# A two-layer decoder on one core: layer 1's expert values as 64 gathered columns and 4 whole chunks, with the list work spread wider

## The chip, the cores and the metric

The kernel runs on one core of a Trainium2 chip. The metric is the device time of one execution in microseconds (us). A core has a matrix engine (TensorE; PE in the profile, with PEld for its weight loads), VectorE (DVE), ScalarE (ACT), GpSimd (POOL) and SyncE (SP). Each engine works through its own list of instructions in order, and semaphores make it wait for the others. SP, ACT and POOL can issue DMA transfers. Products are accumulated in eight PSUM banks; all other data of the engines lie in SBUF.

## What is computed

Input `x` has 256 tokens of width 1024. Each of two layers mixes tokens (layer 0 an mLSTM, layer 1 an RG-LRU, both with cross attention to 256 memory tokens), adds and normalizes, and then applies a mixer of 16384 experts (PEER). The change is about that mixer:

```python
def peer_ffn(x, w_q, subkeys, u_tab, v_tab):      # blocks of 128 tokens
    def block(xb):
        q = (xb @ w_q).reshape(n, PEER_HEADS, 2, PEER_HALF)
        s = jnp.einsum('nhpc,pkc->nhpk', q, subkeys)
        sv, si = lax.top_k(s, PEER_TOPK)
        ...
        fv, fi = lax.top_k(cand.reshape(n, PEER_HEADS, PEER_TOPK * PEER_TOPK), PEER_TOPK)
        eid = ...                                 # ids of 16 experts for each of 8 heads
        gw = jax.nn.softmax(fv, axis=-1)
        act = gelu(jnp.einsum('nhkd,nd->nhk', u_tab[eid], xb))
        return jnp.einsum('nhk,nhkd->nd', gw * act, v_tab[eid])
```

Each token uses 128 of the 16384 experts. Everything is float32, and the tables `u_tab` and `v_tab` hold 16384 rows of 1024 numbers a layer.

## The kernel before

**Tiling.** The experts are 128 chunks of 128 (an expert is a chunk and a partition). A float32 product is made of three faster ones (`mm3`, L310 to L312): high part by high part, high by low and low by high. ACT casts a loaded tile to its high part (L193), and DVE (L208) or POOL (L206) subtracts to get the low part. `pool_cols` says how many columns of it POOL takes.

**First half of the mixer (u).** For every chunk TensorE computes all 256 tokens against its 128 rows of `u` (`u_step`, 256 wide), ACT applies gelu, and DVE multiplies with the gate weights from the top-k selection (L1571). The result, one 128x256 block of coefficients per chunk, stands in `wglo` (chunks 0 to 43) and `wghi` (44 to 127). The chunks of the last 20 steps are called `h` = 64 to 83 in the loop in front of the value phase.

**Second half (v).** The output is the sum over experts of coefficient times row of `v`. Most experts are used by few tokens or none, so the kernel doesn't multiply all 128 chunks. In layer 1 ("joint" in the code) the first `nj` chunks are written to a table in DRAM, `joined`: a row is an expert's 128 coefficients of token block 0, its 1024 values of `v`, and its 128 coefficients of block 1. SP copies the values in, 512 KB a chunk, with every second call of `next` from the first weight load of the kernel on (L286); ACT and SP write the coefficients (`dump`, eight chunks at a time; the two last groups by SP). `lists` (L1142 on) then ranks the used rows of every partition on DVE and writes row numbers to `crow`. A *column* is 128 used rows, one per partition, that one indirect DMA by POOL fetches from `joined` (L248): for one token block 128x1152 numbers, for both 128x1280. There are 15 places for them in `wghi`. Of each partition 16 rows for each block and 8 for both go straight into columns; what is left over (room for `over` rows a partition) is packed into further, "spilled" columns, whose row numbers come from a one-hot product: ten-odd DVE comparisons (L1306) make the one-hots, four left-over rows at a time, and 36 TensorE products (L1313) select. If the left-overs don't fit, a branch computes all chunks in full (`dense`). The chunks from `nj` on are *dense* items: SP loads their whole `v` rows, and they count for both token blocks.

**The value phase.** The loop `for i in range(NC)` takes the items in the order of `value_order`. Item by item ACT casts (L193), DVE subtracts (L208), ACT and DVE split the coefficients (L365, L366), and TensorE multiplies: six products of 128x512 for a token block (two halves of 512 columns, three products each), so six for a single column and twelve for a column of both blocks or a dense chunk. They accumulate in four PSUM banks.

**What sets the order around the change.** Instructions are issued to each engine in the order in which the program writes them. The list work is a generator that is stepped by `tail_lists`: each tick has a budget (`LIST_US` a tick until the rows are ranked, `REST_US` after), and each step is written with the time it takes. A tick comes with every u-step `h` and every value item `i` until the lists are done. Fetching begins when the rows are ranked and the dumps are issued (`self.vrow = self.crow`), and from then on the subtractions go to DVE.

```python
                    self.dumped = n >= len(DUMPS) - 1
                    self.listed = not lists
                    if joint and self.dumped and self.ranked:
                        self.vrow = self.crow
```

Of the kernel before, what the change touches and what calls it, by code (L numbers as in the profile page):

```python
# [7 lines left out]
F32 = mybir.dt.float32  # L8
# [10 lines left out]
P = 128  # L19
# [17 lines left out]
class Shape:  # L37
# [8 lines left out]

    def blocks(self, col):
# [21 lines left out]
SPARE_AT = (P, 14)  # L69
# [10 lines left out]
def value_order(kept, sh):  # L80
    short = list(range(sh.side)) + list(range(sh.a_end, sh.a_end + sh.side))
    short += list(range(sh.side, sh.b_beg)) + list(range(sh.a_end + sh.side, sh.cols))
    both = list(range(sh.b_beg, sh.a_end))
    dense = list(range(sh.nj, P))
    nb = (kept + 1) // 2
    both, last = both[:-nb], both[-nb:]
    dense, spare = dense[:len(dense) - kept + nb], dense[len(dense) - kept + nb:]
    n, ns, cols = len(short) + len(both), len(short), []
    for k in range(n):
        more = (k + 1) * ns // n > k * ns // n  # L90
        cols.append((short if more else both).pop(0))
    out, t = [], 0.0
    for k, c in enumerate(cols):
        while dense and t < sh.first_us + k * sh.pair_us:
            out.append((dense.pop(0), None))
            t += ITEM_US
        t = max(t, sh.first_us + k * sh.pair_us) + ITEM_US * len(sh.blocks(c)) / 2
        out.append((None, c))
    out += [(c, None) for c in dense]
    return out + [(None, last.pop(0)) if k % 2 == 0 else (spare.pop(0), None) for k in reversed(range(kept))]  # L100
# [26 lines left out]
class Trunk:  # L127
# [123 lines left out]
    def fetch(self, dst, col):  # L251
        rows = self.vrow[:, col:col + 1]
        if self.sh.joint:
            n = P * len(self.sh.blocks(col)) + D
# [20 lines left out]
    def next(self, ahead=HL_BUFS):  # L275
# [8 lines left out]
        if self.copying and self.copies and self.calls % 2 == 0:  # L284
# [857 lines left out]
    def lists(self, layer):  # L1142
# [6 lines left out]
        def take(*shape, dt=F32):  # L1149
# [4 lines left out]
            assert at[0] <= (24 if sh.joint else 20) * T  # L1154
            v = v if dt is F32 else v.bitcast(dt)
# [19 lines left out]
        q16, z_in, W = take(OVER, dt=F16), take(OVER, dt=F16), take(OVER, 2, dt=F16)  # L1175
# [118 lines left out]
        nc.vector.tensor_copy(q16, qi2)  # L1294
# [9 lines left out]
        for r in range(0, OVER, 4):  # L1304
            full = [P, 4, P]
            tt_(Q[:, r:r + 4], self.iota2[:, :, 0].unsqueeze(1).to_broadcast(full),  # L1306
                q16[:, r:r + 4].unsqueeze(2).to_broadcast(full), op=ALU.is_equal)
# [33 lines left out]
    def peer_layer(self, layer):  # L1341
# [3 lines left out]
        with ExitStack() as ctx:  # L1345
# [5 lines left out]
            self.crow = wg.tile([P, WIDTH], I32, name="crow")  # L1351
            self.vids = wg.tile([P, WIDTH], I32, name="vids")
# [128 lines left out]
            def tail_lists():  # L1481
                lists = self.lists(layer)
                marks = [c for g in ACT_GROUPS[layer] for c in range(8 * g, 8 * g + 8)]
                budget, n = 0.0, 0
                while True:
                    gain = REST_US if self.ranked else LIST_US
                    budget = min(budget + gain, gain)
                    if n < len(DUMPS):
                        self.dump(nc.scalar, 8 * DUMPS[n], 8, CUT, T)
                    if joint and n in LATE_DUMPS:  # L1490
                        self.dump(nc.sync, 8 * LATE_DUMPS[n], 8, 0, T)
# [12 lines left out]
                    self.dumped = n >= len(DUMPS) - 1  # L1504
# [56 lines left out]
            side = tail_lists()  # L1561
            prev = None
            self.pool_cols, self.chained = D, False
            cs = [] if joint else [coef(0), coef(1)]
            for h in range(NS, NH + 1):
# [9 lines left out]
                if joint and h == NS + 15:  # L1575
# [23 lines left out]
            for i in range(NC):  # L1599
# [3 lines left out]
                if not closed:  # L1603
                    next(side)
# [221 lines left out]
```

## Time and profile before

| | before |
|---|---|
| runs (us) | 1450.7, 1446.2, 1440.04; median 1446.2 |
| the profiled execution (us) | 1449.33 |
| its span (us) | 1447.6 |
| mean TensorE clock granted | 0.996 of full |
| TensorE busy | 1415.5 us |
| DVE busy | 1174.2 us |
| layer 1's value phase | first product at 1302.89, last at 1439.95 |
| block-units there | 50 single columns + 2x12 columns of both + 2x8 dense = 90 |

The span runs from the first to the last instruction of the profiled execution; the device time holds 1.7 us more. Times inside the trace count from the start of the span. In rows of a timeline stand start, duration, engine, line, operation, tiles and count, and in brackets how long the engine idled before it and what ended that. In rows of windows stand, for each stretch, the busy time of TensorE, its weight loads, DVE, ACT and POOL (with instruction counts), the granted clock, the busy share of the DMA engines, and GB/s. In rows of groups stand busy time, mean duration in ns, idle time before, and its releaser.

### The profile page before, as it was taken

The page shows a single profiled execution, that of the slowest core. Times are in us where ns is not written, and L with a number is a line of the kernel's source. Part 1 is how long each engine was busy: PE and PEld are TensorE (multiplying, and loading weights), DVE is VectorE, ACT ScalarE, POOL GpSimd, SP SyncE. Part 2 cuts the span into 40 slices and gives each one's busy share as a digit, 9 for nine tenths or more (in the row PEclk, how much of TensorE's full clock was granted, in tenths as well). Part 3 has the DMA queues.
Part 4 walks back from the last instruction along what each step waited for, and adds up shares of the span by engine and source line. Part 5 has one row for each costly group of instructions (what it writes and reads, how often), then busy time and mean ns, then how long its engine had stood idle before and what let it go on. Part 6 is the DMA issues. An engine that isn't in the chain of part 4 may idle for free. (4 is left out here: it accounts for less than half of the span.)

```text
span 1447.6 us, 30077 instructions
## 1 busy us (share of the span) xinstructions
PE 1415.5 (98%) x11043; PEld 1334.9 (92%) x11043; DVE 1174.2 (81%) x2676; ACT 896.0 (62%) x1937; POOL 592.0 (41%) x500
## 2 busy tenths in 40 slices
PE   8999999999999999999999989999999999998997
PEld 7989999999999999888889879999999999996786
DVE  4667577979999998777886774978899999878986
ACT  4546455555559985566755925555555799845883
POOL 2100665003333349677730136710223323678740
PEclk9999999999999999999999999999999999999999
DMA  8858768887779999889848547788775689997981
GB/s 271 304 201 305 242 228 291 293 287 251 239 248 281 265 242 290 322 301 329 309 152 300 196 150 264 262 291 281 273 239 171 196 261 255 254 321 294 402 342 66
DMA packets 184277, 378.83 MB, mean 262 GB/s; under 512 B 66338, under 2 KB 100140, under 8 KB 183868
## 3 DMA queue, kind: packets, MB, share of 16 engines
q1 hardware_dynamic: 109720, 283.31, 59.2%
q0 software_dynamic: 18608, 69.94, 13.0%
q10 hardware_dynamic: 55796, 23.61, 6.1%
q8 instruction: 88, 1.44, 0.4%
q14 instruction: 65, 0.53, 0.1%
HBM read 346.38 MB, written 93.33 MB: 304 GB/s over the span
## 5 line engine op out<-in xcount | busy, mean ns | idle before, releaser
L310 PE MATMUL bank<-xHL,wH 128*128 128x256 f32 x2536 | 719.3, 284 | 1.9 <-ACT wH L193 1.9
L312 PE MATMUL bank<-xHL,wL 128*128 128x256 f32 x2536 | 708.2, 279 | 6.1 <-DVE wL L208 5.8
L311 PE MATMUL bank<-xHL,wH 128*128 128x256 f32 x2536 | 707.2, 279 | 1.8 <-DVE xHL L366 1.7
L193 ACT CAST wH<-raw 128x1024 fp32r<-128x1024 f32 (+3 forms) x385 | 396.0, 1031 | 369.3 <-PE bank L311 126.8
L312 PEld LDWEIGHTS bank<-xHL,wL 128*128 128x128 f32 x2536 | 478.9, 189 | 9.1 <-DVE wL L208 8.0
L311 PEld LDWEIGHTS bank<-xHL,wH 128*128 128x128 f32 x2536 | 479.3, 189 | 2.6 <-DVE xHL L366 2.6
L310 PEld LDWEIGHTS bank<-xHL,wH 128*128 128x128 f32 x2536 | 477.7, 188 | 2.9 <-ACT wH L193 2.7
L208 DVE TENSOR_TENSOR wL<-raw,wH 128x1024 fp32r<-128x1024 f32 (+3 forms) x186 | 205.5, 1109 | 136.6 <-ACT wH L193 134.4
L206 POOL TENSOR_TENSOR wL<-raw,wH 128x1024 fp32r<-128x1024 f32 (+1 forms) x97 | 212.4, 2194 | 227.2 <-ACT wH L193 225.0
L203 POOL TENSOR_TENSOR wL<-raw,wH 128x386 fp32r<-128x386 f32 x128 | 131.2, 1025 | 291.3 <-DVE wL L201 286.1
L1084 DVE TENSOR_TENSOR oh<-iota,i12T 128x1024 f16<-128x1024 f16 x128 | 138.7, 1084 | 0.0
L312 PE MATMUL bank<-wH,cL 128*128 128x512 f32 (+1 forms) x339 | 133.2, 393 | 2.8 <-DVE cL L366 2.8
L310 PE MATMUL bank<-wH,cH 128*128 128x512 f32 (+1 forms) x339 | 132.7, 391 | 2.8 <-ACT cH L365 2.6
L311 PE MATMUL bank<-wL,cH 128*128 128x512 f32 (+1 forms) x339 | 132.9, 392 | 0.6 <-DVE wL L208 0.6
L201 DVE TENSOR_TENSOR wL<-raw,wH 128x640 fp32r<-128x640 f32 x128 | 105.6, 825 | 14.7 <-ACT wH L193 10.4
L208 DVE TENSOR_TENSOR wL<-wghi,wH 128x1024 fp32r<-128x1024 f32 x66 | 80.8, 1223 | 24.7 <-ACT wH L193 24.6
L248 POOL DMA_INDIRECT wghi<-joined,crow x62 | 85.3, 1376 | 22.5 <-issue 15.5
L1087 DVE TENSOR_TENSOR oh<-oh,gT 128x1024 f16<-128x1024 f16 x128 | 90.0, 703 | 4.4
L193 ACT CAST wH<-wghi 128x1024 fp32r<-128x1024 f32 x66 | 69.3, 1051 | 37.8 <-PE bank L312 25.0
L312 PEld LDWEIGHTS bank<-wH,cL 128*128 128x128 f32 x339 | 63.9, 189 | 19.6 <-DVE cL L366 6.2
L1463 PE MATMUL bank<-oh 128*128 128x128 f16 x1024 | 81.1, 220 | 0.0
L310 PEld LDWEIGHTS bank<-wH,cH 128*128 128x128 f32 x339 | 64.0, 189 | 16.5 <-ACT cH L365 3.1
(371 smaller groups left out, 2095.2 us busy)
## 6 DMA issues: line engine op xcount, KB each, us to landing
raw<-in_u_dram SPq DMA_DIRECT2D x256, 512.0 KB, 4.2
joined<-in_v_dram SPq DMA_DIRECT2D x120, 512.0 KB, 5.5
raw<-in_w_q_dram SPq DMA_DIRECT2D x32, 512.0 KB, 4.0
raw<-in_v_dram SPq DMA_DIRECT2D x20, 512.0 KB, 5.5
raw<-in_w_out_dram SPq DMA_DIRECT2D x16, 512.0 KB, 5.1
raw<-in_w0qx_dram SPq DMA_DIRECT2D x8, 512.0 KB, 5.4
wghi<-in_v_dram SPq DMA_DIRECT2D x8, 512.0 KB, 6.0
raw<-in_w1x_dram SPq DMA_DIRECT2D x8, 512.0 KB, 4.1
```

Source lines behind the costliest of these rows:

```text
L193: (nc.vector.tensor_copy if self.cast_dve else nc.scalar.copy)(h[:, c], r[:, c])
L201: nc.vector.tensor_sub(l[:, k:], r[:, k:], h[:, k:].bitcast(F32))
L203: nc.gpsimd.tensor_sub(l[:, :k], r[:, :k], h[:, :k].bitcast(F32))
L206: nc.gpsimd.tensor_sub(l[:, :k], r[:, :k], h[:, :k].bitcast(F32))
L208: nc.vector.tensor_sub(l[:, k:], r[:, k:], h[:, k:].bitcast(F32))
L248: self.nc.gpsimd.indirect_dma_start(out=dst, out_offset=None, in_=table, in_offset=bass.IndirectOffsetOnAxis(ap=rows, axis=0))
L310: mm(out, sH, mH, start=start, stop=False, skip_group_check=True)
L311: mm(out, sH, mL, start=False, stop=False, skip_group_check=True)
L312: mm(out, sL, mH, start=False, stop=stop, skip_group_check=True)
L1084: nc.vector.tensor_tensor(flat(oh[:, 1:3]), self.iota2.unsqueeze(1).to_broadcast([P, 4, P, 2]), pairs(self.i12T[:, j]), op=ALU.is_equal)
L1087: nc.vector.tensor_tensor(flat(oh[:, 0:2]), two.rearrange("p z (q e t) -> p z q e t", q=2, t=2), pairs(self.gT[:, j]), op=ALU.mult)
L1463: nc.tensor.matmul(wp[:, qs], oh[:, 2, q // 2, :, q % 2], oh[:, z, q // 2, :, q % 2], start=z == 0, stop=z == 1, skip_group_check=True)
```

## The change

**Shape.** `nj` goes from 120 to 124, the room for left-over rows from 36 to 40 a partition, and the spilled columns from (9, 9, 4) to (9, 10, 5): 51 single columns, 13 of both, 4 dense chunks. The list vectors widen from 120 to 124 and from 36 to 40, the comparisons go from 9 to 10, the index products from 36 to 40.

**Order of the value items.** Before: dense 120 and 121, then a column of both and five or six single ones in turn, 122 to 125 at items 61 to 64, and columns of both alternating with dense 126 and 127 at the end. After: dense 124 and 125, then the long items (126, 127 and the columns of both) dealt out evenly among the single ones (one both at item 2, 126 at item 9, the next both at 16, ..., 127 at 49), and at the end six columns of both. The first spilled column is item 40 in both orders.

**Pace of the list work.** `REST_US` is 1.2 instead of 1.0, and in layer 1's value loop the gain is 0.4 with a single column and 1.2 with a long item. The lists end with item 16 instead of 10.

**The comparison's operand.** `q16` (float16, SBUF) becomes `qp` (float32, in a PSUM bank), in both layers.

**Copies.** No copy of `v` into `joined` goes before the 16th call of `next`; four more chunks are copied, so the copying goes on longer in both layers (`COPY_END` 40).

**Dumps and fetching.** SP dumps chunks 120 to 123 as well, in tick 17, and fetching waits for it: it begins in the tick of `h` = 81 instead of 78, and the first coefficient splits come at `h` = 82 instead of 79. Four more marks of used rows fall to ACT, the spare buffers come into use from item 26 instead of 14, and the row numbers of both layers share one tile, `words`.

```diff
-SHAPES = (Shape(104, 16, 8, 28, (5, 6, 3), 5.0, 2.8, False), Shape(120, 16, 8, 36, (9, 9, 4), 3.0, 1.6, True))
-WIDTH = 62
+SHAPES = (Shape(104, 16, 8, 28, (5, 6, 3), 5.0, 2.8, False), Shape(124, 16, 8, 40, (9, 10, 5), 3.0, 1.75, True))
+COPY_AT = 16
+DENSE_FIRST = 10
-LIST_US, REST_US, LOOK = 2.25, 1.0, 10
-ACT_GROUPS = ((5, 9), (5, 9, 13))
+LIST_US, REST_US, LOOK = 2.25, 1.2, 10
+REST_HALF = 0.4
+ACT_GROUPS = ((5, 9), (5, 9, 13, 15))
-LATE_DUMPS = {6: 13, 12: 14}
-COPY_END = 33
+LATE_DUMPS = {6: 13, 12: 14, 17: 15}
+COPY_END = 40
-SPARE_AT = (P, 14)
+SPARE_AT = (P, 26)
...
+    if sh.joint:
+        out = [(dense.pop(0), None) for _ in range(2)]
+        long = [(None, c) for c in cols if len(sh.blocks(c)) == 2]
+        cols = [c for c in cols if len(sh.blocks(c)) == 1]
+        for k in range(len(dense)):
+            long.insert((2 * k + 1) * len(long) // (2 * len(dense)) + k, (dense[k], None))
+        n, m, dense = len(long), len(cols), []
+        for k in range(m):
+            if k * n // m > (k - 1) * n // m:
+                out.append(long.pop(0))
+            out.append((None, cols[k]))
+        out, cols = out + long, []
...
-        if self.copying and self.copies and self.calls % 2 == 0:
+        if self.copying and self.copies and self.calls >= COPY_AT and self.calls % 2 == 0:
...
-        nc.vector.tensor_copy(q16, qi2)
+        qp = self.bank()[:, :OVER]
+        nc.vector.tensor_copy(qp, qi2)
...
-                q16[:, r:r + 4].unsqueeze(2).to_broadcast(full), op=ALU.is_equal)
+                qp[:, r:r + 4].unsqueeze(2).to_broadcast(full), op=ALU.is_equal)
...
-                    gain = REST_US if self.ranked else LIST_US
-                    budget = min(budget + gain, gain)
+                    gain = self.gain if self.ranked else LIST_US
+                    budget = min(budget + gain, max(gain, REST_US))
...
-                        self.dump(nc.sync, 8 * LATE_DUMPS[n], 8, 0, T)
+                        self.dump(nc.sync, 8 * LATE_DUMPS[n], min(8, NJ - 8 * LATE_DUMPS[n]), 0, T)
...
-                    self.dumped = n >= len(DUMPS) - 1
+                    self.dumped = n >= (max(LATE_DUMPS) if joint else len(DUMPS) - 1)
...
-                if joint and h == NS + 15:
+                if joint and h == NJ - N0 + 2:
                     cs = [coef(0), coef(1)]
...
+                    if joint:
+                        self.gain = REST_HALF if len(blocks(order[i][1])) == 1 else REST_US
                     next(side)
```

**Where instructions move: the value phase's start on DVE.** `wL<-raw` is the low part of a loaded chunk, `wL<-wghi` that of a gathered column, `cL` that of coefficients, `wghi<-wghi,bank` the gate product of a u-step, and `wglo<-iota` a comparison. Before, from the last but one u-step on:

```order
L1571 TENSOR_TENSOR wghi<-wghi,bank 128x256
L1306 TENSOR_TENSOR wglo<-iota_93,wglo 128x512 x2
L1571 TENSOR_TENSOR wghi<-wghi,bank 128x256
L208 TENSOR_TENSOR wL<-wghi,wH 128x1024
L1306 TENSOR_TENSOR wglo<-iota_93,wglo 128x512
L366 TENSOR_TENSOR cL<-wghi,cH 128x256
L208 TENSOR_TENSOR wL<-wghi,wH 128x1024
L1306 TENSOR_TENSOR wglo<-iota_93,wglo 128x512
L366 TENSOR_TENSOR cL<-wghi,cH 128x128
L208 TENSOR_TENSOR wL<-wghi,wH 128x1024
```

After, at the same place (line numbers are some 20 higher):

```order
L1594 TENSOR_TENSOR wghi<-wghi,bank 128x256
L1323 TENSOR_TENSOR wglo<-wglo 128x40x24
L1327 TENSOR_TENSOR wglo<-iota_93,bank 128x512
L1594 TENSOR_TENSOR wghi<-wghi,bank 128x256
L227 TENSOR_TENSOR wL<-wghi,wH 128x1024
L1327 TENSOR_TENSOR wglo<-iota_93,bank 128x512
L386 TENSOR_TENSOR cL<-wghi,cH 128x256
L227 TENSOR_TENSOR wL<-wghi,wH 128x1024
L1327 TENSOR_TENSOR wglo<-iota_93,bank 128x512 x2
L386 TENSOR_TENSOR cL<-wghi,cH 128x128
L227 TENSOR_TENSOR wL<-wghi,wH 128x1024
```

The comparisons read a bank instead of `wglo`, and one stands before the last gate product where three stood; the rest have moved in among the columns.

**Where fetching begins, on SP.** `joined<-wghi` are the late dumps, `raw<-in_u` and `raw<-in_v` loads of chunks. Before, at the end of layer 1's u loads:

```order
L1136 DMA joined<-wghi 128x8x128 x2
L243 DMA raw<-in_u_dram 128x1024 x6
L1136 DMA joined<-wghi 128x8x128 x2
L243 DMA raw<-in_v_dram 128x1024 x6
L1633 TENSOR_LOAD go
```

After:

```order
L1156 DMA joined<-wghi 128x8x128 x2
L262 DMA raw<-in_u_dram 128x1024 x6
L1156 DMA joined<-wghi 128x8x128 x2
L262 DMA raw<-in_v_dram 128x1024 x2
L1156 DMA joined<-wghi 128x4x128 x2
L262 DMA raw<-in_v_dram 128x1024 x2
L1658 TENSOR_LOAD go
```

A third pair of dumps stands behind the first two loads of dense chunks. On POOL the gathers follow a run of subtractions (`wL<-raw`), ten before and thirteen after.

**The start, on SP.** Before, from the tenth instruction of the program (loads of the first projection, and copies of `v`):

```order
L243 DMA raw<-in_xT_dram 128x256
L243 DMA raw<-in_w0kg_dram 128x896
L243 DMA raw<-in_xT_dram 128x256
L286 DMA joined<-in_v_dram 128x1024
L243 DMA raw<-in_w0kg_dram 128x896
L243 DMA raw<-in_xT_dram 128x256
L243 DMA raw<-in_w0kg_dram 128x896
```

After:

```order
L262 DMA raw<-in_xT_dram 128x256
L262 DMA raw<-in_w0kg_dram 128x896
L262 DMA raw<-in_xT_dram 128x256
L262 DMA raw<-in_w0kg_dram 128x896
L262 DMA raw<-in_xT_dram 128x256
L262 DMA raw<-in_w0kg_dram 128x896
```

The first copy, and those behind it up to the loads of `w0v`, have left this stretch.

More of the change, by code (lines that the diff above doesn't have):

```diff
@@ L45, in __init__, with spilled @@
         self.nc = P - nj + self.cols
+    def spilled(self, col):
+        return self.side <= col < self.b_beg or self.b_beg + self.mid <= col < self.a_end or col >= self.a_end + self.side
     def blocks(self, col):
         return (0, 1) if col is None or self.b_beg <= col < self.a_end else (0,) if col < self.b_beg else (1,)
-SHAPES = (Shape(104, 16, 8, 28, (5, 6, 3), 5.0, 2.8, False), Shape(120, 16, 8, 36, (9, 9, 4), 3.0, 1.6, True))
-WIDTH = 62
+SHAPES = (Shape(104, 16, 8, 28, (5, 6, 3), 5.0, 2.8, False), Shape(124, 16, 8, 40, (9, 10, 5), 3.0, 1.75, True))
+COPY_AT = 16
+DENSE_FIRST = 10
 ITEM_US = 2.73
@@ L84, in value_order @@
     dense = list(range(sh.nj, P))
-    nb = (kept + 1) // 2
+    nb = max((kept + 1) // 2, 2 * kept - len(dense) + DENSE_FIRST) if sh.joint else (kept + 1) // 2
+    nb = min(nb, kept)
     both, last = both[:-nb], both[-nb:]
@@ L99, in value_order @@
     out += [(c, None) for c in dense]
-    return out + [(None, last.pop(0)) if k % 2 == 0 else (spare.pop(0), None) for k in reversed(range(kept))]
+    return out + [(None, last.pop(0)) if k % 2 == 0 or k >= 2 * len(spare) else (spare.pop(0), None)
+                  for k in reversed(range(kept))]
 def value_homes(layer):
@@ L253, in fetch @@
         if self.sh.joint:
+            assert self.listed or not self.sh.spilled(col)
             n = P * len(self.sh.blocks(col)) + D
@@ L1153, in take @@
             at[0] += w
[L1154 to L1155 removed]
+            assert at[0] <= (28 if sh.joint else 20) * T
+            v = v if dt is F32 else v.bitcast(dt)[:, :n]
             if len(shape) == 2:
@@ L1174, in lists @@
         si, qi2, qz = take(OVER, dt=I32), take(OVER, dt=I32), take(OVER)
-        q16, z_in, W = take(OVER, dt=F16), take(OVER, dt=F16), take(OVER, 2, dt=F16)
+        z_in, W = take(OVER, dt=F16), take(OVER, 2, dt=F16)
         Z = take(OVER, SPILL, dt=F16)
@@ L1350, in peer_layer @@
             self.junk = wg.tile([P, P], F16, name="junk")
-            self.crow = wg.tile([P, WIDTH], I32, name="crow")
-            self.vids = wg.tile([P, WIDTH], I32, name="vids")
+            words = wg.tile([P, 2 * SHAPES[0].nj + 2 * SHAPES[0].cols + 6 - 2 * NJ], I32, name="words")
+            self.crow = words[:, 0:COLS]
+            self.vids = None if joint else words[:, COLS:2 * COLS]
             self.go = wg.tile([P, 1], I32, name="go")
@@ L1482, in tail_lists @@
                 lists = self.lists(layer)
-                marks = [c for g in ACT_GROUPS[layer] for c in range(8 * g, 8 * g + 8)]
+                marks = [c for g in ACT_GROUPS[layer] for c in range(8 * g, min(8 * g + 8, NJ))]
                 budget, n = 0.0, 0
                 while True:
-                    gain = REST_US if self.ranked else LIST_US
-                    budget = min(budget + gain, gain)
+                    gain = self.gain if self.ranked else LIST_US
+                    budget = min(budget + gain, max(gain, REST_US))
                     if n < len(DUMPS):
@@ L1561, in peer_layer @@
             side = tail_lists()
+            self.gain = REST_US
             prev = None
```

## The prediction, made before the changed kernel ran

> **What bounds the kernel now.** I read the page first: busy time per engine, and the groups of the value phase (the products of layer 1's second half).
>
> ```profile
> PE 1415.5 (98%) x11043; PEld 1334.9 (92%) x11043; DVE 1174.2 (81%) x2676; ACT 896.0 (62%) x1937; POOL 592.0 (41%) x500
> L312 PE MATMUL bank<-wH,cL 128*128 128x512 f32 (+1 forms) x339 | 133.2, 393 | 2.8 <-DVE cL L366 2.8
> L248 POOL DMA_INDIRECT wghi<-joined,crow x62 | 85.3, 1376 | 22.5 <-issue 15.5
> ```
>
> TensorE is busy 98% of the span, so work taken off it counts in full, and another engine's time counts only where TensorE stands still. The gathers idle 15.5 us for "issue": something holds them that no semaphore shows. Next I read the windows of the value phase (busy us of PE, PEld, DVE, ACT, POOL; then clock, DMA share, GB/s).
>
> ```profile
> 1290.00:1300.00 10.00, 9.55 (x80) 9.15 (x80) 9.69 (x35) 4.37 (x7) 5.53 (x4) 1.00 0.81 292
> 1310.00:1315.00 5.00, 4.97 (x22) 3.67 (x20) 5.00 (x9) 2.65 (x6) 5.00 (x1) 1.00 0.53 213
> 1315.00:1320.00 5.00, 4.73 (x53) 3.58 (x52) 5.00 (x9) 2.51 (x4) 5.00 (x1) 1.00 0.01 3
> 1320.00:1325.00 5.00, 3.40 (x15) 2.43 (x13) 0.30 (x1) 0.26 (x1) 3.93 (x4) 1.00 0.62 198
> 1325.00:1330.00 5.00, 3.40 (x8) 2.22 (x8) 2.89 (x5) 3.38 (x6) 3.94 (x4) 0.70 0.98 373
> 1350.00:1400.00 50.00, 50.00 (x216) 40.39 (x217) 45.62 (x65) 41.13 (x64) 37.39 (x34) 1.00 1.02 412
> ```
>
> From 1350 on TensorE never waits. Between 1315 and 1330 it does, right after five microseconds in which the DMA engines moved nothing. The timelines of POOL, ACT and TensorE say why.
>
> ```profile
> 1284.88 4.77 POOL L206 TENSOR_TENSOR wL<-raw,wH 128x1024 fp32r<-128x1024 f32 x2 [1.81 <-ACT wH L193]
> 1293.56 1.62 POOL L248 DMA_INDIRECT wghi<-joined,crow  x1 [3.91 <-DMA raw<-in_v_dram]
> 1306.31 1.23 POOL L248 DMA_INDIRECT wghi<-joined,crow  x1 [0.30 <-issue]
> 1307.84 13.27 POOL L248 DMA_INDIRECT wghi<-joined,crow  x1 [0.30 <-issue]
> 1321.41 0.94 POOL L248 DMA_INDIRECT wghi<-joined,crow  x1 [0.30 <-issue]
> 1324.74 1.04 ACT L193 CAST wH<-wghi 128x1024 fp32r<-128x1024 f32 x1 [6.54 <-DMA wghi<-joined,crow]
> 1302.89 0.40 PE L310 MATMUL bank<-wH,cH 128*128 128x512 f32 x1
> 1319.04 0.40 PE L310 MATMUL bank<-wH,cH 128*128 128x512 f32 x1
> 1323.00 0.40 PE L312 MATMUL bank<-wH,cL 128*128 128x512 f32 x1
> 1326.03 0.49 PE L310 MATMUL bank<-wH,cH 128*128 128x512 f32 x1 [2.64 <-ACT cH L365]
> 1336.29 0.51 PE L312 MATMUL bank<-wH,cL 128*128 128x512 f32 x1 [0.71 <-DVE cL L366]
> 1346.90 0.50 PE L312 MATMUL bank<-wH,cL 128*128 128x512 f32 x1 [0.54 <-DVE cL L366]
> ```
>
> The eighth gather took 13.27 us, where the ninth took 0.94. The next rows landed late, ACT waited 6.54 us for them, and TensorE 2.64 us. The clock then fell to 0.70. What DVE did meanwhile:
>
> ```profile
> 1306.64 0.41 DVE L1571 TENSOR_TENSOR wghi<-wghi,bank 128x256 f32<-128x256 f32 x1
> 1306.97 1.22 DVE L208 TENSOR_TENSOR wL<-wghi,wH 128x1024 fp32r<-128x1024 f32 x1
> 1308.11 0.69 DVE L1306 TENSOR_TENSOR wglo<-iota,wglo 128x512 f16<-128x512 f16 x1
> 1308.71 0.42 DVE L366 TENSOR_TENSOR cL<-wghi,cH 128x256 fp32r<-128x256 f32 x1
> 1310.79 0.28 DVE L366 TENSOR_TENSOR cL<-wghi,cH 128x128 fp32r<-128x128 f32 x1
> 1319.88 0.42 DVE L366 TENSOR_TENSOR cL<-wghi,cH 128x256 fp32r<-128x256 f32 x1
> ```
>
> From 1306.97 to 1320.30 DVE was busy without a pause, with operations that read two operands from SBUF. The seventh gather ended (1307.54) 0.90 us after the start of L1571, which has one operand in a PSUM bank. The eighth began behind the last such operation and ended (1321.11) 0.81 us after DVE fell idle. So I read the stall as POOL's descriptor work held off by DVE's two-operand reads.
>
> **The change, part by part.**
>
> Fewer block-units. A unit is one token block of one item: 6 products of 128x512. From 1319.04 to 1323.00 stand 17 steps, 0.233 us each, so a unit is 1.40 us. Before there are 50 single and 12 double columns and 8 dense chunks: 50 + 24 + 16 = 90 units; after, 51 + 26 + 8 = 85. That removes 30 products: **-7.0 us**, all on TensorE. Loading keeps up: three quarters of the items are still single columns, and 1350 to 1400 shows them at full TensorE rate, with longer items to catch up.
>
> The gather stall. From 1323.00 to 1336.29 TensorE issued 27 products, worth 6.3 us, in 13.3 us; 0.7 more went before 1346.90. The stall costs 7.7 us. The edit for it: the one-hot comparison (L1306 before) reads its second operand from a PSUM bank, so ten of DVE's operations there now have one SBUF operand; they are spread to item 16 instead of 10 by smaller gains for single columns. If the reading above holds, each lets a gather through: **-7.7**.
>
> What is late next. Fetching waits for the dump of chunks 120 to 123 and starts in the tick of step 81 instead of 78. A step is 2.8 us (3 us by 1290 to 1300, with its wait), so 8.4 us later in the code, though not all on the chip, for POOL was done at 1289.65 and stood 3.91 us for a DMA. POOL also keeps three more subtractions of some 2.39 us (half of 4.77), one per step, so it is free at about 1289.65 + 8.4 = 1298.1, which is where I put the first gather, 4.5 us later than now. Its rows land 6.8 us after issue by this row of the DMA issues from 1290 to 1330:
>
> ```profile
> wghi<-joined,crow POOLq DMA_INDIRECT x15, 6.8
> ```
>
> That is 1304.9, and 1306 with the cast of 1.04. TensorE wants the first column (item 2) at 1302.89 + 4 units = 1308.5: 2.5 us to spare. From then on DVE is the tight one: a single column costs it a subtraction of 1.14 us (1306.97 to 1308.11) and a coefficient part of 0.28 at most, about TensorE's 1.40, and each comparison 0.6 (1308.11 to 1308.71) more. Up to item 10 DVE has nine subtractions, nine coefficient parts and eight comparisons, 17 us from 1306, that is to 1323; TensorE has one double column, six single ones and a dense chunk, ten units or 14 us from 1308.5, that is to 1322.5. So DVE ends half a microsecond behind, and each wait on the way costs a little. Bounds: 0.5 (one gap like the 0.54) to 6 (the first gather 3.5 later, or a shorter stall). I take **+2.5**, nearer to the small waits of 0.5 to 0.7 in the rows, some four of them.
>
> The start. Seven copies of v into the joined table left the first 55 us.
>
> ```profile
> 10.00:15.00 5.00, 4.16 (x32) 3.56 (x31) 2.70 (x4) 1.50 (x3) 0.00 (x0) 1.00 0.82 233
> 15.00:20.00 5.00, 4.41 (x38) 4.22 (x38) 1.44 (x3) 2.17 (x4) 0.00 (x0) 1.00 0.92 348
> 20.00:25.00 5.00, 4.44 (x39) 4.25 (x38) 2.86 (x4) 1.68 (x4) 0.00 (x0) 1.00 0.96 288
> 25.00:30.00 5.00, 2.66 (x21) 2.27 (x20) 2.02 (x2) 2.71 (x3) 0.00 (x0) 0.99 0.99 367
> 30.00:35.00 5.00, 5.00 (x32) 5.00 (x32) 3.07 (x4) 3.00 (x7) 0.00 (x0) 0.67 0.85 267
> 35.00:40.00 5.00, 5.00 (x46) 5.00 (x46) 0.79 (x4) 1.68 (x6) 1.31 (x1) 1.00 0.93 279
> 18.34 0.51 SPq L286 DMA_DIRECT2D joined<-in_v_dram  x1
> 18.95 0.53 SPq L243 DMA_DIRECT2D raw<-in_w0kg_dram  x1
> 26.75 0.94 ACT L193 CAST wH<-raw 128x896 fp32r<-128x896 f32 x1 [4.22 <-DMA raw<-in_w0kg_dram]
> ```
>
> Between 10 and 30 TensorE idles 4.3 us, and from 30 to 35 the clock of 0.67 costs 14 products of 0.11 us, 1.5 more: 5.8 at most. The load of 18.95 stands behind a copy and kept ACT waiting to 26.75. Three copies of 0.5 MB are a quarter of the 6.2 MB that these four windows moved at a DMA share of 0.82 to 0.99. Lower bound nothing (loads late by their own latency, as at 10 to 15 with share 0.82), upper 5.8. I take **-3.5**, since the worst window is the one at 0.99.
>
> Small parts. DVE subtracts three fewer in the last steps, so the 0.45 us that TensorE lost from 1290 to 1300 goes: **-0.4**. Four more index products, at 0.03 each (1.07 us for 36): **+0.1**. Four more marks and wider list vectors: nothing, ACT is busy 62%. Moved and added copies: SP issues them behind the same loads, three more at the end of the copying in layer 0 and eight in layer 1.
>
> ```profile
> 440.00:445.00 5.00, 5.00 (x50) 4.96 (x49) 4.96 (x12) 4.78 (x21) 1.84 (x2) 1.00 1.06 385
> 1100.00:1125.00 25.00, 25.00 (x243) 24.65 (x241) 23.64 (x44) 13.12 (x29) 7.54 (x8) 1.00 0.47 150
> 1316.65 1.07 PE L1313 MATMUL bank<-wglo 128*128 128x44 f16 x36
> ```
>
> In layer 1 they hide under a share of 0.47. In layer 0 TensorE stayed busy even at 1.06; without that cover three copies would cost up to 4 us. I take 0.
>
> **Sum.** -7.0 - 7.7 + 2.5 - 3.5 - 0.4 + 0.1 = -16.0. The profiled execution took 1449.3 (span 1447.6), so 1433.3 there. It lies 3.1 above the median of the runs, 1446.2, and that gives **1430**.
>
> **Rivals.**
>
> A: The PSUM operand frees nothing, and the gather starves as before. For it: L1306 is only one in three of DVE's operations there, and L208 and L366 still read two. Against it: seven gathers got through while L1571 came between. The 7.7 stays in place of 2.5: 1435.
>
> The Trainium skill, page "SBUF — State Buffer", section "Who interferes with whom", speaks for A: a DVE operation with two SBUF inputs contends with GpSimd's reads and not its writes, and descriptors are inferred to need only writes. By that the stall has another cause, the edit misses it, and the sum would be A's 1435. The 13.27 us under nothing but such operations don't agree with it, but no run here shows the cause alone.
>
> B: The late start becomes the wait. With all 8.4 us of it the first gather goes at 1302.0, lands at 1308.8 and is cast at 1309.9, 1.4 late, with no slack for what follows, so 3 to 4 more than forecast: 1433.5. Against it is the idle time of 3.91 before the first gather now. With A on top: 1439.
>
> C: The start gives nothing, as loads are late by latency alone: 1433.5.
>
> D, the other side: POOL and DVE alternate all through the longer list. The first seven gathers took 14 us, 2.0 each; at that pace the fourteenth column (item 16), wanted twenty units after 1302.89, at 1330.9, is there at 1298.1 + 26 + 7.8 = 1331.9, 1 us late. At 3.3 each it is 18 late and the gain is gone; at 4 each it is 27 late, and the time 1455. Against it: only one interval but the stalled one passes 3 us.
>
> E: The left-over rows don't fit the room of 40, and the branch computes all chunks again: over 124 dense items of 2.8, 350 us more. Four added chunks add at most one row each to a partition's left-overs, and 36 held them before, so the room holds. I leave it at under 1 in 100.
>
> **Chances.** Forecast 0.58 (its own range 1424 to 1434), A 0.17, B 0.10, C 0.10, D and E 0.05. Low end: the start at 5.8 and the residual at 0.5 give 1425.7, and 2 of spread. High end: A with B, 1439, and 2. A measurement of this kernel tells about 1% from no change, that is under 1431.7 or over 1460.7. Three quarters of the forecast's chance lie under 1431.7, with a little of C and B: faster 0.46. Slower 0.03, same 0.51.
>
> **What would show it.** Products of 128x512 down by 30. The longest gather of layer 1 under 4 us and DMA never idle from 1300 to 1320; a gather of 8 us or more under busy DVE makes A right. First gather some 4 to 5 us nearer to the first product than now; if ACT's first cast of a column waits and TensorE with it, B. Windows 10 to 30 with TensorE at 18 or more of 20, and no clock below 0.9 after; if not, C. I am wrong altogether if TensorE shows new idle time in layer 0, which I priced at nothing.

## The result, and the profile after

| | before | after |
|---|---|---|
| median of 14 runs each (us) | 1442.87 | 1436.01 |
| lowest to highest (us) | 1438.79 to 1450.70 | 1431.84 to 1440.24 |
| ratio of after to before | | 0.9948, 95% interval 0.9934 to 0.9963 |
| profiled execution (us) | 1449.33 | 1434.09 |

The change made the kernel faster by 0.52% (0.37 to 0.66), or 7.5 us of 1442.87 (the two medians lie 6.9 apart). That is inside the range of 1423 to 1441, but less than half of the 16 us forecast, and it falls in the case "within 1%", which had 0.51. The two profiled executions differ by 15.2 us, close to the 16.0 forecast; that agreement is an accident, as the further profiles of the kernel before show. The forecast of 1430 also started from a median of three runs, 1446.2, which lies 3.3 above that of the fourteen.

The page of the changed kernel, first the engines, then the groups of the value phase and the gathers:

```profile
PE 1404.8 (98%) x11017; PEld 1324.1 (92%) x11017; DVE 1171.2 (82%) x2673; ACT 894.9 (62%) x1949; POOL 591.4 (41%) x505
...
L332 PE MATMUL bank<-wH,cL 128*128 128x512 f32 (+1 forms) x345 | 136.6, 396 | 4.7 <-DVE cL L386 4.7
...
L267 POOL DMA_INDIRECT wghi<-joined,words x64 | 75.0, 1172 | 24.2 <-issue 13.7
```

The group of L332 (products of both layers) holds 345 now (339 before), though fewer are needed: more of them use the `wH` buffers and fewer the spare ones, since those come into use at item 26. All 128x512 products from the value phase's start on are 492 against 522, the 30 that the prediction counted. The wait for `cL` rose from 2.8 to 4.7 us.

Windows of the changed kernel from the first gather on (busy time of PE, PEld, DVE, ACT, POOL; clock, DMA share, GB/s):

```profile
1290.00:1295.00 5.00, 5.00 (x47) 5.00 (x46) 4.76 (x18) 1.73 (x3) 2.75 (x3) 1.00 0.98 298
1295.00:1300.00 5.00, 3.06 (x16) 2.26 (x15) 4.97 (x8) 1.89 (x4) 4.09 (x4) 1.00 0.96 347
1300.00:1305.00 5.00, 4.99 (x22) 3.73 (x21) 4.59 (x7) 3.02 (x5) 3.92 (x4) 1.00 1.02 406
1305.00:1310.00 5.00, 4.09 (x17) 2.67 (x16) 5.00 (x9) 3.32 (x6) 3.92 (x4) 1.00 1.02 413
1310.00:1315.00 5.00, 4.77 (x21) 3.54 (x20) 5.00 (x8) 3.58 (x6) 3.81 (x4) 1.00 1.02 408
1315.00:1320.00 5.00, 4.37 (x19) 2.93 (x18) 5.00 (x9) 2.77 (x5) 4.39 (x3) 1.00 1.02 412
```

The DMA engines no longer fall idle. Yet TensorE stands still again: 1.9 us at once where the value phase begins (1295.33), and in small pieces up to 1320, with DVE busy for 4.97 to 5.00 us of each such 5. TensorE's and DVE's timelines at the first item:

```profile
1295.56 0.40 PE L331 MATMUL bank<-wL,cH 128*128 128x512 f32 x1
1297.90 0.50 PE L332 MATMUL bank<-wH,cL 128*128 128x512 f32 x1 [1.94 <-DVE cL L386]
...
1295.12 1.15 DVE L1320 TENSOR_TENSOR wglo<-wglo 128x960 f16<-128x960 f16 x1
1296.31 1.16 DVE L1323 TENSOR_TENSOR wglo<-wglo 128x960 f16<-128x960 f16 x1
1297.39 0.79 DVE L386 TENSOR_TENSOR cL<-wghi,cH 128x256 fp32r<-128x256 f32 x2
```

The first item's third product needs the low part of its coefficients. That subtraction (L386) stands on DVE behind two list steps of 1.15 us, and TensorE waits for it.

The start, 10 to 30 us, in the changed kernel:

```profile
10.00:30.00 20.00, 20.00 (x172) 20.00 (x171) 12.12 (x15) 11.07 (x18) 0.00 (x0) 1.00 0.88 290
```

TensorE is busy all 20 us, against 15.7 in the profile of before. These two are the ends of the range: the further profiles below have 18.3 to 19.1 there with late copies and 16.6 to 18.3 with early ones.

### The profile page after: what moved, and what is told of

It reads as the page before. It is cut to its first block, busy times and chain, and to the rows that moved or that the text cites. A ratio compares the mean times of both kernels' runs of the same rounds, so it can differ in the third digit from the quotient of the medians.

```text
span 1432.1 us, 30025 instructions
## 1 busy us (share of the span) xinstructions
PE 1404.8 (98%) x11017; PEld 1324.1 (92%) x11017; DVE 1171.2 (82%) x2673; ACT 894.9 (62%) x1949; POOL 591.4 (41%) x505
## 5 line engine op out<-in xcount | busy, mean ns | idle before, releaser
L332 PE MATMUL bank<-xHL,wL 128*128 128x256 f32 x2536 | 705.8, 278 | 2.6 <-DVE wL L227 2.3
L332 PEld LDWEIGHTS bank<-xHL,wL 128*128 128x128 f32 x2536 | 479.4, 189 | 3.9 <-DVE wL L227 2.9
L225 POOL TENSOR_TENSOR wL<-raw,wH 128x1024 fp32r<-128x1024 f32 (+1 forms) x100 | 219.4, 2200 | 222.8 <-ACT wH L212 220.8
L227 DVE TENSOR_TENSOR wL<-raw,wH 128x1024 fp32r<-128x1024 f32 (+3 forms) x183 | 201.7, 1106 | 129.4 <-ACT wH L212 129.2
L332 PE MATMUL bank<-wH,cL 128*128 128x512 f32 (+1 forms) x345 | 136.6, 396 | 4.7 <-DVE cL L386 4.7
L330 PE MATMUL bank<-wH,cH 128*128 128x512 f32 (+1 forms) x345 | 135.9, 394 | 0.1
L227 DVE TENSOR_TENSOR wL<-wghi,wH 128x1024 fp32r<-128x1024 f32 x71 | 86.8, 1222 | 19.7 <-ACT wH L212 19.4
L212 ACT CAST wH<-wghi 128x1024 fp32r<-128x1024 f32 x71 | 74.5, 1049 | 34.4 <-PE bank L332 28.7
L332 PEld LDWEIGHTS bank<-wH,cL 128*128 128x128 f32 x345 | 64.7, 187 | 23.7 <-DVE cL L386 8.5
L267 POOL DMA_INDIRECT wghi<-joined,words x64 | 75.0, 1172 | 24.2 <-issue 13.7
L331 PEld LDWEIGHTS bank<-wL,cH 128*128 128x128 f32 x345 | 64.7, 187 | 15.8
```

What stands on the lines that cost most here:

```text
L212: (nc.vector.tensor_copy if self.cast_dve else nc.scalar.copy)(h[:, c], r[:, c])
L225: nc.gpsimd.tensor_sub(l[:, :k], r[:, :k], h[:, :k].bitcast(F32))
L227: nc.vector.tensor_sub(l[:, k:], r[:, k:], h[:, k:].bitcast(F32))
L267: self.nc.gpsimd.indirect_dma_start(out=dst, out_offset=None, in_=table, in_offset=bass.IndirectOffsetOnAxis(ap=rows, axis=0))
L330: mm(out, sH, mH, start=start, stop=False, skip_group_check=True)
L331: mm(out, sH, mL, start=False, stop=False, skip_group_check=True)
```

## The experiments

Every ratio is to the kernel before, run in the same comparison. "Lost time" of the value phase is what the longer distances (over 0.26 us) between starts of neighbouring 128x512 products exceed 0.2325 us, summed from the first to the last of them; the stretch of the index products is left out.

### Is the stall of the first profile the rule? The kernel before, twice more

No edit.

> The kernel before, unchanged, for a second profile. In the first one a gather took 13.27 us and the value phase of layer 1 took 137.1 us (first to last product), 8.2 more than with the comparison's operand in PSUM, while the median time of that version is only 2.1 us lower. My theory: the stall is not in every execution, so this profile shows a longest gather under 6 us and a value phase of 129 to 132 us. Rival: the stall is always there; gather over 10 us and 136 to 138 us again.

> The kernel before, unchanged, for a third profile; the same two theories as for the second (longest gather under 6 us and value phase 129 to 132 us, or over 10 us and 136 to 138 us). If the two profiles differ from each other, the stall comes and goes.

The two profiled executions took 1439.69 and 1441.94 us. Gathers of POOL and DVE's operations beside them, in the second profile of the kernel before:

```profile
1311.86 1.25 POOL L248 DMA_INDIRECT wghi<-joined,crow  x1 [0.30 <-issue]
1313.41 1.63 POOL L248 DMA_INDIRECT wghi<-joined,crow  x1 [0.30 <-DMA wghi<-joined,crow]
1315.35 1.63 POOL L248 DMA_INDIRECT wghi<-joined,crow  x1 [0.30 <-DVE cL L366]
...
1313.02 1.22 DVE L208 TENSOR_TENSOR wL<-wghi,wH 128x1024 fp32r<-128x1024 f32 x1
1314.15 0.68 DVE L1306 TENSOR_TENSOR wglo<-iota,wglo 128x512 f16<-128x512 f16 x1
1314.76 0.28 DVE L366 TENSOR_TENSOR cL<-wghi,cH 128x128 fp32r<-128x128 f32 x1
1314.96 1.22 DVE L208 TENSOR_TENSOR wL<-wghi,wH 128x1024 fp32r<-128x1024 f32 x1
1316.09 0.28 DVE L366 TENSOR_TENSOR cL<-wghi,cH 128x128 fp32r<-128x128 f32 x1
```

No gather passes 2.5 us in either profile. From 1313.02 to 1316.37 DVE runs without a pause through the very operations that were to starve a gather, and two gathers of 1.63 us begin and one ends in that time. The value phase takes 128.94 and 128.90 us from its first to its last product instead of 137.06, and loses 1.4 us in each instead of 9.7. So the stall came in one profile of three. That it is rare fits the timed runs, though they don't show their gathers: of the 54 of the kernel before in the first three comparisons, five took 1447.9 us or more. The reading that two-operand reads on DVE hold gathers off is not a rule, and the cause of that one gather of 13.27 us stays open.

### The comparison's operand: back to SBUF, and alone in the kernel before

The changed kernel with the float16 operand, in both layers:

```diff
...
-        qp = self.bank()[:, :OVER]
-        nc.vector.tensor_copy(qp, qi2)
+        nc.vector.tensor_copy(q16, qi2)
...
-                qp[:, r:r + 4].unsqueeze(2).to_broadcast(full), op=ALU.is_equal)
+                q16[:, r:r + 4].unsqueeze(2).to_broadcast(full), op=ALU.is_equal)
```

> The changed kernel, with the comparison's operand back in SBUF as float16. My theory: the gathers starve again as long as DVE runs two-operand SBUF reads back to back; the longest gather in layer 1 is over 7 us, DMA falls idle between 1295 and 1320, and the time rises by 4 to 9 us. Rival (the stall has another cause, or the new order and pace removed it): the longest gather stays under 4 us and the time within 1 us of the changed kernel.

Median 1435.39 us, ratio 0.9950 (0.9932 to 0.9968); the changed kernel has 0.9948. No gather passes 2.5 us, and the lost time is 8.2 us (8.7 in the changed kernel).

The kernel before with this edit made the other way round:

> The kernel before, with only the comparison's operand moved to a PSUM bank in both layers. My theory: the 13 us gather goes (longest under 4 us), DMA never idles between 1310 and 1320, and the time falls by 4 to 8 us against the kernel before. Rival one: the gather starves all the same (longest over 8 us), no difference. Rival two: the gathers come through, but DVE, which is behind its work in this stretch, then makes TensorE wait instead, and the time falls by less than 3 us.

Median 1440.59 us, ratio 0.9983 (0.9966 to 1.0000), that is 2.5 us or nothing. Its value phase takes 128.89 us and loses 1.4, just as the further profiles of before do without the edit. Its expectation compared it with the first profile, and rests on the same mistake. Together the two runs show no difference by the operand's place that is clear of the noise; the second leaves room for one of up to 0.34%, 5 us.

### The first coefficient splits ahead of the list steps

```diff
+                if joint and h == NJ - N0 + 2:
+                    cs = [coef(0), coef(1)]
                 if h < NH:
                     next(side)
                 prev = g
-                if joint and h == NJ - N0 + 2:
-                    cs = [coef(0), coef(1)]
```

> The changed kernel, but at step 82 the first two coefficient splits are written ahead of that tick's list steps. My theory: the changed kernel loses 2.1 us at its first value product because the low parts of the first two items' coefficients stand on DVE behind two list steps of 1.15 us each, so this version should be 1.5 to 2.1 us faster than it, and the wait of 1.94 us before the first item's third product should be gone. Rival: DVE is short of time in this whole stretch, so the two list steps only delay the next subtractions, the wait reappears by item 2 to 8, and the time stays within 0.7 us of the changed kernel.

Median 1434.41 us, ratio 0.9940 (0.9916 to 0.9964), 1.6 us under the changed kernel's median of the other comparison; the intervals overlap, so the gain itself isn't sure. TensorE's timeline at the third item:

```profile
1304.43 0.49 PE L331 MATMUL bank<-wL,cH 128*128 128x512 f32 x1 [0.40 <-DVE wL L227]
1305.36 0.50 PE L332 MATMUL bank<-wH,cL 128*128 128x512 f32 x1 [0.44 <-DVE cL L386]
```

And its waits from 1290 to 1355, those of the changed kernel, and those of the second profile of before (engine, line, what it waited for; us in total, times, longest):

```profile
PE bank L332 <- DVE cL L386: 3.6, 8, 0.7
PE bank L331 <- DVE wL L227: 0.6, 2, 0.4
```

```profile
PE bank L332 <- DVE cL L386: 5.4, 8, 1.9
```

```profile
PE bank L312 <- DVE cL L366: 0.5, 1, 0.5
```

The wait at the first item is gone, as the first theory has it. At the third item 0.84 us of it comes back, as the rival has it: the value phase shrinks from 128.78 to 127.57 us, and the lost time from 8.7 to 7.5. The rest reads as a lack of DVE time over the whole stretch to item 16, where DVE is busy all the time. The kernel before has 0.5 us of such waits there.

### The copies from the start again

```diff
-COPY_AT = 16
+COPY_AT = 0
```

> The changed kernel, with the copies of v from the start again. My theory: the first 30 us lose what the profile of before lost there, so TensorE is busy 16 to 17 of the 20 us from 10 to 30 and the time is 3 to 5 us higher. Rival: the loads of the start are late in some executions only and the mean gain is small; then the time is within 1.5 us of the changed kernel although this profile may show idle time at the start.

Median 1437.27 us, ratio 0.9966 (0.9950 to 0.9981). In the same comparison the two versions with late copies have 0.9940 and 0.9950, so the copies at the start cost 0.16 to 0.26%, 2.3 to 3.7 us, and the intervals overlap. The profile, itself the slowest of the twelve runs (1443.69), shows more:

```profile
10.00:30.00 20.00, 16.63 (x131) 15.35 (x130) 9.52 (x13) 8.32 (x12) 0.00 (x0) 1.00 0.89 301
L330 PE MATMUL bank<-wH,mixH x40: 277/389/583, 123.2 to 852.8; 128*128 128x512 f32 x24, 128*128 128x256 f32 x16
```

The first product with the mixer's output, 116.8 in the changed kernel, comes at 123.2, 6.4 us later. A second profile:

> The changed kernel with the copies from the start again, a second profile. In the first one the first product with the mixer's output came 6.4 us later than in the changed kernel, while the median of the runs is only 1.3 to 2.9 us higher. If the loss at the start is there in every execution, this profile has it too (6 us); if it varies, the first product comes 0 to 4 us later.

It comes at 124.3 there, in a comparison in which every kernel took longer (1461.78 us for the kernel before). But in the same comparison two versions with late copies, described below, have it at 117.4 and 118.6. Over all profiles the six with early copies have 122.0 to 124.3, and the eight with late ones 116.1 to 118.6. So the loss at the start is there in every profile, 5.8 us on average; why the timed runs differ by only 2 to 4 us stays open.

### Why layer 0 became slower and layer 1 faster: where the tiles lie

The profiles showed a thing that no term of the prediction holds. With the same products, TensorE busy throughout and the clock at 1.00, their number in a stretch differs. The second profile of before, then the changed kernel: a stretch of layer 0's u-steps, of its value phase, and of layer 1's u-steps.

```profile
350.00:400.00 50.00, 50.00 (x494) 49.47 (x492) 48.40 (x92) 27.92 (x62) 15.32 (x15) 1.00 0.74 245
650.00:700.00 50.00, 50.00 (x222) 41.36 (x222) 39.84 (x57) 34.80 (x55) 39.33 (x36) 1.00 0.92 320
1050.00:1100.00 50.00, 50.00 (x477) 49.34 (x476) 47.16 (x90) 26.70 (x61) 15.33 (x15) 1.00 0.71 227
```

```profile
350.00:400.00 50.00, 50.00 (x486) 49.41 (x485) 47.79 (x93) 26.82 (x60) 15.59 (x16) 1.00 0.73 237
650.00:700.00 50.00, 50.00 (x216) 40.18 (x215) 38.53 (x55) 33.49 (x54) 39.90 (x34) 1.00 0.90 311
1050.00:1100.00 50.00, 50.00 (x486) 49.42 (x485) 47.89 (x93) 27.16 (x61) 15.42 (x16) 1.00 0.70 235
```

A single step is steadier than such counts. The starts of the one-hot products of neighbouring u-steps in layer 0 of the changed kernel:

```profile
400.88 0.64 PE L1485 MATMUL bank<-oh 128*128 128x128 f16 x8
404.24 0.64 PE L1485 MATMUL bank<-oh 128*128 128x128 f16 x8
407.50 0.64 PE L1485 MATMUL bank<-oh 128*128 128x128 f16 x8
410.86 0.64 PE L1485 MATMUL bank<-oh 128*128 128x128 f16 x8
```

Steps of 3.36 and 3.26 us in turn, in both layers; the one-hots use two buffers in turn. In the kernel before all 64 steps of layer 0 take 3.267 and (but for a first one in one profile) all of layer 1 3.357. A fast step has its products 113.3 ns apart. In layer 0's value phase they stand 226.6 ns apart before and 233.3 after. What differs is where tiles lie: the change packs two tables into one tile, and `wghi` with all that follows starts at byte 91424 of a partition in both layers, where it started at 91456 in layer 0 and at 91584 in layer 1. An unused tile of 32 bytes brings it to 91456:

```diff
             self.go = wg.tile([P, 1], I32, name="go")
+            wg.tile([P, 8], F32, name="shift")
```

> The changed kernel with an unused tile of 32 bytes a partition in front of wghi, so that wghi and what lies behind it start where they start in layer 0 of the kernel before (offset 91456 instead of 91424). In layer 0 of before a u-step of the 64 takes 3.267 us, in its layer 1 (offset 91584) 3.357, and in the changed kernel 3.36 and 3.26 in turn in both layers. My theory: the place in SBUF sets the rate; with this shift all 128 steps take 3.267 us, which is 5.6 us in all, layer 0's value products stand 226.7 ns apart instead of 233.3 (4 us), and the time falls by 5 to 10 us against the changed kernel. Rival: the rate is not set by the place, the steps stay at a mean of 3.31, and the time stays within 1 us.

Median 1427.89 us, ratio 0.9881 (0.9853 to 0.9910): the first version that is faster than before by over 1%, and below the changed kernel's interval. Its windows:

```profile
350.00:400.00 50.00, 50.00 (x495) 49.43 (x494) 48.45 (x91) 27.10 (x61) 15.73 (x16) 1.00 0.74 242
650.00:700.00 50.00, 50.00 (x222) 41.39 (x221) 40.62 (x57) 35.66 (x55) 39.33 (x36) 1.00 0.93 326
1050.00:1100.00 50.00, 50.00 (x493) 49.47 (x490) 48.37 (x92) 27.94 (x63) 15.28 (x15) 1.00 0.74 244
```

All u-steps of layer 0 and all but four of layer 1 (3.36 to 3.41) take 3.267 us, and layer 0's value products stand 226.7 ns apart. Only the one-hots moved:

```diff
+                octx.enter_context(tc.tile_pool(name=f"ohs{layer}", bufs=1)).tile([P, 8], F32, name="shift")
                 self.ohp = octx.enter_context(tc.tile_pool(name=f"oh{layer}", bufs=2))
```

> The changed kernel with the unused 32 bytes between wghi and the one-hot tiles only, so that the one-hots start where they start in layer 0 of before and wghi stays where the change put it. If the one-hots' place sets the rate of the u-steps, all take 3.267 us in this profile; if wghi's place does, they stay at 3.36 and 3.26 in turn.

One profile, 1430.94 us. The u-steps take 3.267 us in both layers (but for five of layer 1), and layer 0's value products stay 233.3 ns apart (216 from 650 to 700). So the one-hots' place sets the rate of the steps that use them, though the 24 other products of a step read nothing there. All other profiles fit: a place of the one-hots goes with one pattern of steps in each of them. In the value phase it is something else that the whole shift moves, `wghi` or the coefficient tiles behind it. And it isn't place alone: in layer 1's first u-loop, which has no one-hots, the profile with the whole shift has 853 products from 900 to 1000, and the changed kernel 885, but two profiles of one and the same kernel, the last one of the next section, have 857 and 882.

### Less DVE work at the start of the value phase

Shift, early splits, and the gain with a single column down to 0.25:

```diff
-REST_HALF = 0.4
+REST_HALF = 0.25
```

> The changed kernel with the 32 byte shift, the first two coefficient splits ahead of the list steps, and the gain with a single column at 0.25 instead of 0.4, so that the comparisons lie thinner among the columns. My theory: the 7 us that the value phase of layer 1 loses more than before's are DVE work placed too late and too thick; with both moves its lost time falls from 8.6 us to 4 to 6, and the total is 2 to 4 us below the version with the shift alone (1427.9). Rival: DVE has the same work in the same 25 us whatever its order, so the lost time stays above 7 us and the total within 1 us of the shift alone.

And all four dense chunks first:

```diff
-        out = [(dense.pop(0), None) for _ in range(2)]
+        out = [(dense.pop(0), None) for _ in range(4)]
```

> The same, with all four dense chunks at the start of the value phase instead of two there and two among the columns. A dense chunk gives TensorE 2.8 us and DVE only about 1.5, so two more of them give DVE 2.6 us and push the first column's need back by 5.6 us. My theory: the lost time of the value phase falls by another 2 to 3 us, to 1.5 to 3, and the total with it. Rival: the columns then lack long items later, loading at 1.43 us for 1.40 of work falls behind, and as much is lost after 1350 as was won.

> The version with the shift, the early coefficient splits, the thinner comparisons and all four dense chunks first, once more, because in the last comparison transfers were slow for every kernel (the kernel before took 1461.8 us there against 1442.7 and 1444.3 in the two comparisons ahead of it) and the waits of its value phase were waits for loads. Where the kernel before takes about 1443 again: the lost time of the value phase is 1.5 to 4 us instead of the 8.6 of the version with the shift alone, the DVE waits at the first item and at items 3 to 8 are gone, and the time is 1420 to 1425, a ratio of 0.984 to 0.988. Rival: DVE's work is only moved, the lost time stays above 7 us, and the ratio is 0.987 to 0.990, as with the shift alone (0.9881).

| | median (us) | before, same comparison | ratio |
|---|---|---|---|
| thinner list steps | 1460.63 | 1461.78 | 0.9981 (0.9954 to 1.0009) |
| and four dense first | 1455.00 | 1461.78 | 0.9943 (0.9921 to 0.9965) |
| the same again | 1466.35 | 1470.97 | 0.9960 (0.9926 to 0.9994) |

These don't answer the question. The kernel before, 1442.7 to 1444.3 in the comparisons ahead, took 18 to 28 us more here. TensorE also stood still in both layers' value phases, in the first of these profiles for "issue" (a wait for nothing that the profile shows) and for coefficient casts (once 3.7 us), which the profiles of the changed kernel and of the shift don't have; what held it isn't shown. Four dense chunks first took 5.6 us less than two in the same comparison, and their profile loses 14.2 us in layer 1's value phase against 18.8, but the two intervals overlap. Whether either beats the shift alone when the kernel before takes 1443 stays open.

## Why the prediction was right and wrong

The time lies in the range, for the wrong sum. Four points of the program stand in every profile, and the time between them can be compared: the first and the last product with the mixer's output (layer 0 and layer 1), and the first and the last of layer 1's value phase. The second profile of before, then the changed kernel:

```profile
L310 PE MATMUL bank<-wH,mixH x40: 277/389/583, 122.0 to 845.6; 128*128 128x512 f32 x24, 128*128 128x256 f32 x16
1301.40 0.39 PE L310 MATMUL bank<-wH,cH 128*128 128x512 f32 x1
```

```profile
L330 PE MATMUL bank<-wH,mixH x40: 276/389/586, 116.8 to 846.4; 128*128 128x512 f32 x24, 128*128 128x256 f32 x16
1295.33 0.39 PE L330 MATMUL bank<-wH,cH 128*128 128x512 f32 x1
```

| stretch (us) | before, second profile | before, third | after | difference |
|---|---|---|---|---|
| to the mixer's output, layer 0 | 122.0 | 122.6 | 116.8 | -5.2, -5.8 |
| to the same in layer 1 | 723.6 | 726.8 | 729.6 | +6.0, +2.8 |
| to layer 1's first value product | 455.8 | 454.3 | 448.9 | -6.9, -5.4 |
| value phase | 128.9 | 128.9 | 128.8 | -0.1 |
| span | 1438.0 | 1440.2 | 1432.1 | -5.9, -8.1 |

**Fewer units, -7.0.** Right as a count: 492 products for 522. In the value phase next to nothing of it is left (128.9 to 128.8), because of the third term.

**The stall, -7.7.** The first step that failed. It read one execution as the kernel. Two more profiles of before have no such gather and a value phase 8 us shorter, so in those executions there was nothing to remove. The PSUM operand, which was to remove it, changes nothing that is clear of the noise by two timed runs. In that half rival A was right: the operand frees nothing that was seen. The Trainium skill, page "SBUF — State Buffer", section "Who interferes with whom", infers that a `tensor_tensor` with both inputs in SBUF doesn't hold up descriptors. The second profile agrees: gathers of 1.63 us go through under such operations.

**What is late next, +2.5.** The second step that failed. The mechanism was half right: DVE is short of time up to item 16, and the first gathers come in time. The size was not: lost time went from 1.4 to 8.7 us, 7.3 more, past the bound of 6. The first gather came 2.6 us ahead of the first product, where the first profile of before has 9.3: 6.8 later, and 4.5 was forecast. Still TensorE's waits behind it were for DVE, and not for columns as rival B had it. Two things were not priced.

The first coefficient splits moved to step 82, as the section on the change says, and there they queue behind that step's list work: 2.1 us.

And four more marks fall to ACT, which the prediction put at nothing because ACT has time. But the ranking begins when the last mark is written, and the program writes three in a step: 28 marks take ten steps, and 24 took eight. So the ranking begins two steps later. These rows show DVE idle in front of it, and where the row numbers are written, in the second profile of before and then in the changed kernel:

```profile
1265.96 0.42 DVE L1571 TENSOR_TENSOR wghi<-wghi,bank 128x256 f32<-128x256 f32 x1 [2.24 <-ACT bank L1570]
1268.78 0.42 DVE L1571 TENSOR_TENSOR wghi<-wghi,bank 128x256 f32<-128x256 f32 x1 [2.40 <-ACT bank L1570]
1287.99 0.33 DVE L1273 TENSOR_SCALAR crow<-wglo 128x16 int32<-128x16 f32 x3
```

```profile
1261.26 0.42 DVE L1594 TENSOR_TENSOR wghi<-wghi,bank 128x256 f32<-128x256 f32 x1 [1.92 <-ACT bank L1593]
1263.96 0.42 DVE L1594 TENSOR_TENSOR wghi<-wghi,bank 128x256 f32<-128x256 f32 x1 [2.29 <-ACT bank L1593]
1266.68 0.42 DVE L1594 TENSOR_TENSOR wghi<-wghi,bank 128x256 f32<-128x256 f32 x1 [2.30 <-ACT bank L1593]
1269.40 0.42 DVE L1594 TENSOR_TENSOR wghi<-wghi,bank 128x256 f32<-128x256 f32 x1 [2.30 <-ACT bank L1593]
1290.90 0.33 DVE L1293 TENSOR_SCALAR words<-wglo 128x16 int32<-128x16 f32 x3
```

Two such idle steps became four, and the row numbers come 4.4 us ahead of the first product instead of 13.4. List work that lay beside u-steps so lies in the value phase. No run tried fewer marks on ACT or more of them in a step, so what this alone costs is not shown. On top of it, the work ahead of the ranking ran into POOL's subtractions. DVE and POOL in the changed kernel:

```profile
1285.58 2.40 DVE L1276 CAST wglo<-wglo 128x40 f16<-128x40 f32 x1
1278.23 9.70 POOL L225 TENSOR_TENSOR wL<-raw,wH 128x1024 fp32r<-128x1024 f32 x4 [1.21 <-ACT wH L212]
```

A cast of 40 elements a partition took 2.40 us, until the fourth of POOL's subtractions was over (1287.93); in the profiles of before the same cast, of 36, took 0.18. The same section of the Trainium skill says that `cast` and `tensor_scalar` can enter modes in which they need the port pair that DVE shares with GpSimd, and that whoever comes second waits for the other's whole instruction. This trace agrees. The kernel before has such a wait too: its three `tensor_scalar` just ahead of the cast took 2.14 us together in the second profile, and the same three took 2.32 after. What is new is the cast's 2.2 us, and 0.6 at a `tensor_scalar` behind it (1.47 us for 0.86).

**The start, -3.5.** Right in direction, and in size between the two measures: 5.2 and 5.8 us by the profiles, 2.3 to 3.7 by the timed version with early copies. Six of the seven copies left the first 55 us, and one stayed, at 51.3. Rival C fell.

**Layer 0, nothing.** Wrong, though not by the sign that the prediction named: TensorE shows no new idle time there, it is slower while busy. The 63 distances between u-steps grew by 0.044 us each (2.8 us), and some 600 value products by 6.7 ns (4.0 us, of which 3.3 is left at the next of the four points). In layer 1, also put at nothing, the same effect has the other sign: 63 times 0.046, 2.9 us, 1.9 in the loop ahead of them and 2.1 in the steps behind. Against the second profile the two nearly cancel, so the effect explains the shape of the table, not the total.

The sum with the measured terms is -7.0 + 7.3 - 5.2 + 6.0 - 6.9 = -5.8 against the second profile of before, where the spans differ by 5.9. That the time lies in the range is luck: the gain of 7.7 wasn't there, and the waiting was 4.8 more than forecast. Against that stand only 1.7 more at the start and 0.9 that layer 1 won beyond layer 0's loss; for the rest, the median that the forecast started from was 3.3 too high, and the range was wide enough.

## What to carry to other kernels

Take a second profile before a single long instruction becomes a term of the sum: the spread of three runs (10.7 us) was larger than that term, and a stall in one execution is not yet the kernel's. When work leaves one engine at a stage's end, ask what the stage's control work has to wait for because of it: here four more chunks in the table took 7 us of products off TensorE, four more marks made the ranking wait two steps, and 7 us of waiting for DVE came in their place. And when tiles change size, compare the product rate of busy stretches in both profiles, since busy time alone hides it.

## What the runs showed of the hardware that was not expected

TensorE's products run at one of two rates with the clock at 1.00 and no wait shown: 113.3 or about 118 ns apart at 256 columns, 226.6 or 233.3 at 512. A rate holds for hundreds of microseconds or changes from step to step, and 32 bytes of unused SBUF changed it in nearly all of the 128 u-steps. By the profiles that shift took 2.8 and 2.3 us off the two layers' u-steps and 4.3 off layer 0 from its value phase on. In that profile layer 1 lost 5.7 up to its u-steps, in a loop whose rate also differs between two profiles of the same kernel, and the span fell by 4.0. The medians stand 8.1 apart. Why the place of the one-hots slows products that don't read them was not found.

One gather took 13.27 us in one profile of three of the same kernel. No other profile has one over 3.6, but for one of 5.85 in the last. What held it is open too.
